# An encoder block whose attention products move one tile back, and two of whose attention outputs skip the trip through memory

## The chip, the core and the metric

The kernel runs on one core of one Trainium2 chip. The core has five engines with an instruction queue each: PE (matrix products), DVE and POOL (element-wise work), ACT (copies, exponentials, sigmoids) and SP, which here only issues transfers. An engine works off its queue in the order in which the program stands there, and waits on semaphores that the other engines and the transfers set. The metric is the device time of the whole program in microseconds (us); lower is better.

## The reference, cut to what matters

One encoder layer on 1024 tokens of width 1024:

```
a = rms_norm(x)
qa, ka, va, qd, kd, vd, gate_na, gate_dil = split(a @ w_in)
y_na  = neighborhood_attention(qa, ka, va)          # 8 heads of 64, 64-wide token grid
y_dil = dilated_attention(rotary(qd), rotary(kd), vd)   # 3 groups x 4 heads, groups merged per head
mixed = sigmoid(gate_na) * (y_na @ W_A) + sigmoid(gate_dil) * (y_dil @ W_B)
h = x + mixed @ W_o
h = h + relu(rms_norm(h) @ W_up)**2 @ W_down
h = h + sigmoid(rms_norm(h) @ W_g) * (p @ W_p)
out = rms_norm(h)
```

Everything is float32. The kernel gets that precision by splitting each operand into a rounded part and a remainder ("h" and "l", or "hi" and "lo") and adding up products of the parts.

## The kernel before

The program is written once, unrolled, and a scheduler puts the instructions of each engine in order by a simulated clock; only PE in the attention part, and a few marked instructions, keep the order in which they are written. Its stages: projections of q, k and v (0 to about 380 us of the span), attention (to about 725 us), the branch products with W_A and W_B (to about 810 us), then W_o, the MLP and the last gated embedding.

**The attention loop.** There are 160 tiles: 96 of the dilated attention (six pairs of heads, 16 tiles each), then 64 of the neighbourhood attention (eight heads, 8 tiles each). A tile is 128 queries of one head. For tile i the loop emits: the three scores ahead, that is the score product of tile i+3 (`na_score`, `dil_score`, lines 637 and 638, into a `sc` bank); the softmax of it on DVE (`soft`, `soft_max`, lines 644 to 655), ACT (the exponential, lines 647 and 657) and for the neighbourhood tiles POOL (`na_norm`, line 722, which scales the `s_sb` tile); the transposes of tile i on PE (`na_turn`, `dil_turn`, lines 731 and 860 to 866, into a `tp_p` bank), whose result ACT copies to `pt_h` and DVE subtracts to `pt_l` (`split`, lines 109 and 110). Two neighbourhood tiles, or four dilated ones, make a group; behind the last transposes of a group comes its product with v (`na_av`, lines 753 and 754, or `dil_av`, lines 900 and 903, into the single `av` bank), which needs all its `pt_h` and `pt_l`. ACT copies the upper half of that bank to `fold` (lines 762 and 908) and DVE adds it (lines 766 and 909) into the output tile, `y_na` or `numer`.

In iteration i PE is given, in this order: the transposes of tile i; some products of the gate projections (`ps_g`, line 602), dealt out as filler by `pay`; the scores of tile i+3; the product with v of a group that ended with tile i-1 (`late`); filler again; and the steps that were put off with `later`.

**Transfers around it.** All are issued by SP in one queue. `v_t` holds the v of a pair of heads (three buffers); `dil_v` loads its first part with the first score of a pair and its second part (`part` 1) in the turn of that pair's tile 1. `bias` has the neighbourhood bias. The four outputs of the neighbourhood attention (`y_na`, a tile for two heads) and the two merged outputs of the dilated attention (`y_d`, built by `dil_out` in three steps from `nm_d` and `fb_d`, tag `md`, two buffers, lines 964 and 968) share the tag `y` with two buffers. Each is stored to `y_scr` when it is done.

**The branch products.** Behind the loop the remaining filler runs; then all six outputs are loaded back from `y_scr` in the order 4, 5, 0, 1, 2, 3 (0 to 3 are the neighbourhood ones, 4 and 5 the dilated ones) into `y_raw` tiles of tag `y`, and split into the pairs `y_op` by ACT (line 109) and DVE (line 110). PE multiplies them with the branch weights (`ps_b`, lines 208 to 210): 288 products of 128x512, eight blocks f of output features by two halves of the tokens, 6 products for branch B (outputs 4 and 5) and 12 for branch A (0 to 3) in each. The gates come back from memory into `gt` tiles (the first half of the tokens in tag `bias`, the second in tag `md`); ACT takes the sigmoid, DVE multiplies `ps_b` by it (line 1058), and the `ps_b` bank is free only then (three banks).

Of the kernel before, what the change touches and what calls it, by code (L numbers as in the profile page):

```python
# [9 lines left out]
F32 = mybir.dt.float32  # L10
# [7 lines left out]
P = 128  # L18
S = 1024
# [13 lines left out]
AHEAD = 3  # L33
# [26 lines left out]
def encoder_kernel(ctx: ExitStack, tc: tile.TileContext, t: dict, out: bass.AP):  # L60
    nc = tc.nc
# [373 lines left out]
    with ExitStack() as st:  # L435
# [10 lines left out]
        raw, flips = {}, [0]  # L446
# [135 lines left out]
    with ExitStack() as st:  # L582
# [82 lines left out]
        def later(n, f):  # L665

            after.setdefault(now[0] + n, []).append(f)
# [66 lines left out]
        def na_av(h, cb, env):  # L734
            j, e = h // 2, h % 2
            pth, ptl = env.pop(("pt", cb))
            i_ = cb % 2
            if i_ == 0:
                env["av"] = ps_av.tile([P, 2, 256], F32, name="av", tag="av")
            av = env["av"]  # L740
            vh = [env["vt"][:, i_, gq, :] for gq in range(4)]
            first = True
            for gq, i, c in ((1, 0, None), (2, 1, None), (0, 2, 0), (3, 2, 1)):
                last = gq == 3
                if c is None:
                    mh = pth[:, i].rearrange("p a b -> p (a b)")
                    ml = ptl[:, i].rearrange("p a b -> p (a b)")
                    oc = slice(0, 256)
                else:
                    mh, ml = pth[:, i, c, :], ptl[:, i, c, :]  # L750
                    oc = slice(c * P, (c + 1) * P)
                m = P if last else 64
                pe(nc.tensor.matmul(av[:, i_, oc], vh[gq], mh, start=first, stop=False))
                pe(nc.tensor.matmul(av[0:m, i_, oc], vh[gq][:, 0:m], ml, start=False, stop=last))
                first = False
            if i_ == 0:
                return
            if e == 0 and cb == 1:
                na_y[j] = ap.tile([P, S], F32, name="y_na", tag="y")
            y = na_y[j]  # L760
            tmp = ap.tile([64, HALF], F32, name="fold", tag="fold", bufs=1)
            nc.scalar.copy(tmp, av[64:128].rearrange("p a b -> p (a b)"))
            for a in range(2):
                c = cb - 1 + a
                dst = y[e * 64:(e + 1) * 64].rearrange("p (r c) -> p r c", c=GW)[:, :, c * 16:(c + 1) * 16]
                nc.vector.tensor_tensor(dst, av[0:64, a].rearrange("p (r c) -> p r c", c=16),
                                        tmp[:, a * 256:(a + 1) * 256].rearrange("p (r c) -> p r c", c=16), op=ALU.add)
            if e == 1 and cb == 3:
                later(2, lambda: nc.sync.dma_start(y_scr[j], y))

        env_head = {}
# [73 lines left out]

        def dil_turn(g_, pr_, e, qi, pair, env):
            half, qp, qq = qi // 4, qi % 4 // 2, qi % 2
            if e == 0 and qi == 1:
                dil_v(g_, pr_, pair, 1)
            if qi % 4 == 0:  # L850
                env["pt"] = tuple(ap.tile([P, 8, P], F32R, name=f"pt_{b}", tag=f"pt_{b}") for b in "hl")
            if qq == 0:
                env["tp"] = ps_tp.tile([P, 4, P], F32, name="tp_p", tag="tp")
            pth, ptl = env["pt"]
            tp, pr = env["tp"], env.pop(("pr", qi))
            k0, n, _ = window(g_, qi)
            if g_ == 0:

                a0 = qi * P + 64 - k0
                pe(nc.tensor.transpose(tp[0:a0, 2 * qq, :], pr[:, 0:a0], ident))  # L860
                pe(nc.tensor.transpose(tp[0:n - a0, 2 * qq + 1, :], pr[:, a0:n], ident))
            elif g_ == 1:
                for b in range(2):
                    pe(nc.tensor.transpose(tp[:, 2 * b + qq, :], pr[:, b * P:(b + 1) * P], ident))
            else:
                pe(nc.tensor.transpose(tp[:, qq, :], pr[:, :P], ident))
            if qq == 0:
                return

            o0 = 4 * qp  # L870
            if g_ == 2:
                parts = ((2 * qp, 0, 2, P),)
            elif g_ == 0 and half == 0 and qp == 0:
                parts = ((o0, 0, 1, 64), (o0 + 1, 1, 3, P))
            elif g_ == 0 and half == 1 and qp == 1:
                parts = ((o0, 0, 3, P), (o0 + 3, 3, 1, 64))
            else:
                parts = ((o0, 0, 4, P),)
            for o, i, m, hh in parts:
                split(pth[:hh, o:o + m, :], ptl[:hh, o:o + m, :], tp[:hh, i:i + m, :])  # L880
# [71 lines left out]
        def dil_out(pr_, g_=0, y=None):  # L952

            y = y or ap.tile([P, S], F32, name="y_d", tag="y")
            nm = ap.tile([P, S], F32, name="nm_d", tag="md", bufs=2)
            nc.sync.dma_start(nm, n_scr[2 * g_ + pr_])
            fb = ap.tile([P, S], F32, name="fb_d", tag="md", bufs=2)
            for e in range(2):
                s_ = 2 * pr_ + e
                nc.sync.dma_start(fb[e * 64:(e + 1) * 64], f_scr[g_, s_:s_ + 1, :].broadcast_to((64, S)))  # L960

            def scaled():
                dst, a, b = (y, nm, fb) if g_ == 0 else (tok_view(fb, g_), nat_view(nm, g_), tok_view(fb, g_))
                tc.keep_in_program_order(nc.vector.tensor_tensor(dst, a, b, op=ALU.mult))

            def added():
                if g_:
                    tc.keep_in_program_order(nc.vector.tensor_tensor(y, y, fb, op=ALU.add))
                if g_ < 2:
                    dil_out(pr_, g_ + 1, y)  # L970
                else:
                    later(2, lambda: nc.sync.dma_start(y_scr[4 + pr_], y))

            later(5, scaled)
            later(6, added)
# [31 lines left out]
        for h in range(8):  # L1007
# [2 lines left out]
                after.setdefault(len(tiles) - 8, []).append(dil_merge)  # L1010
            elif h in (3, 5):
                after.setdefault(len(tiles) - (8 if h == 3 else 3), []).append(lambda pr_=h // 2 - 1: dil_out(pr_))
        late, i = None, -AHEAD
        while i <= len(tiles) or any(n >= i for n in after):
            if 0 <= i + AHEAD - 1 < len(tiles) and tiles[i + AHEAD - 1][0][3]:
                tiles[i + AHEAD - 1][0][3]()
            if 0 <= i < len(tiles):
# [3 lines left out]
            if i + AHEAD < len(tiles):  # L1021
                tiles[i + AHEAD][0][0]()
            now[0] = i
            if late:
                late()
            late = tiles[i][0][2] if 0 <= i < len(tiles) else None
            for f in after.pop(i, ()):
                f()
            pay(1.0)
# [7 lines left out]
            + [(ap, "pt_l", 2)] * 2  # L1037
        yt = {}
        for i, k in enumerate((4, 5, 0, 1, 2, 3)):
            raw = ap.tile([P, S], F32, name="y_raw", tag="y")  # L1040
            nc.sync.dma_start(raw, y_scr[k])
            yh, yl = (pool.tile([P, S], F32R, name="y_op", tag=tag, bufs=bufs)
                      for pool, tag, bufs in (spots[2 * i], spots[2 * i + 1]))
            split(yh, yl, raw)
            yt[k] = (yh, yl)
# [503 lines left out]
```

## Time and profile before

| | |
|---|---|
| time, median of three runs | 1675.5 us (1675.15, 1675.5 and one of 7496.38) |
| the profiled execution | 1673.03 us, span 1670.8 us |
| PE busy | 1571.5 us, 94% of the span |
| DVE, ACT, POOL busy | 1200.9, 708.4, 654.0 us |
| mean granted PE clock | 0.974 of full speed |
| moved by the transfers | 279.22 MB, 167 GB/s over the span |

The span runs from the first instruction to the last; the device time holds 2.2 us more. Two of the three runs agree within 0.35 us, and the third stands alone at more than four times that time. PE's busy time is modelled and includes time at the lower clock, so that 94% does not say that 6% is all that can be won. The full clock is 2.4 GHz and the lower level 1.2 GHz; a granted clock of 0.5 in a window means the lower level throughout.

### The profile page before, as it was taken

The page shows a single profiled execution, that of the slowest core. Times are in us where ns is not written, and L with a number is a line of the kernel's source. Part 1 is how long each engine was busy: PE and PEld are TensorE (multiplying, and loading weights), DVE is VectorE, ACT ScalarE, POOL GpSimd, SP SyncE. Part 2 cuts the span into 40 slices and gives each one's busy share as a digit, 9 for nine tenths or more (in the row PEclk, how much of TensorE's full clock was granted, in tenths as well). Part 3 has the DMA queues.
Part 4 walks back from the last instruction along what each step waited for, and adds up shares of the span by engine and source line. Part 5 has one row for each costly group of instructions (what it writes and reads, how often), then busy time and mean ns, then how long its engine had stood idle before and what let it go on. Part 6 is the DMA issues. An engine that isn't in the chain of part 4 may idle for free. (4 is left out here: it accounts for less than half of the span.)

```text
span 1670.8 us, 22589 instructions
## 1 busy us (share of the span) xinstructions
PE 1571.5 (94%) x7787; PEld 1312.3 (79%) x7787; DVE 1200.9 (72%) x2081; ACT 708.4 (42%) x1327; POOL 654.0 (39%) x434
## 2 busy tenths in 40 slices
PE   8899999999999998879997899999989999999997
PEld 7899777787787877757886688888877788887886
DVE  6744799734665788645557776777778999999955
ACT  7322222216787666644334333333345333333422
POOL 0233678613333222215304677777742322225100
PEclk9999999999999999989998999999999999999999
DMA  8552455674566778556343344434467454433122
GB/s 309 169 156 103 138 161 160 208 266 165 189 197 217 230 224 275 182 189 183 139 164 126 107 140 139 145 139 146 145 222 277 156 167 161 143 111 128 43 101 70
DMA packets 115058, 279.22 MB, mean 167 GB/s; under 512 B 14240, under 2 KB 30592, under 8 KB 114432
## 3 DMA queue, kind: packets, MB, share of 16 engines
q1 hardware_dynamic: 109184, 267.29, 48.7%
q10 hardware_dynamic: 5760, 10.49, 1.7%
q8 instruction: 62, 1.02, 0.3%
q14 instruction: 52, 0.43, 0.1%
HBM read 186.61 MB, written 91.11 MB: 166 GB/s over the span
## 5 line engine op out<-in xcount | busy, mean ns | idle before, releaser
L109 ACT CAST w_hi<-w_raw 128x512 fp32r<-128x512 f32 (+2 forms) x103 | 83.7, 826 | 144.4 <-POOL w_raw L470 55.9
L110 POOL TENSOR_TENSOR w_lo<-w_raw,w_hi 128x512 fp32r<-128x512 f32 (+2 forms) x33 | 64.2, 1947 | 154.5 <-ACT w_hi L109 150.5
L110 DVE TENSOR_TENSOR f_lo<-f_raw,f_hi 128x512 fp32r<-128x512 f32 x80 | 81.7, 1039 | 52.0 <-ACT f_hi L109 51.3
L110 DVE TENSOR_TENSOR w_lo<-w_raw,w_hi 128x1024 fp32r<-128x1024 f32 (+1 forms) x70 | 85.2, 1224 | 37.7 <-ACT w_hi L109 37.5
L722 POOL TENSOR_SCALAR s_sb<-s_sb,rs 128x384 f32<-128x384 f32 x64 | 41.3, 645 | 134.1 <-DVE rs L721 88.9
L109 ACT CAST f_hi<-f_raw 128x512 fp32r<-128x512 f32 x80 | 46.1, 613 | 82.9 <-DMA f_raw<-w_up 79.7
L110 DVE TENSOR_TENSOR pt_l<-tp_p,pt_h 128x384 fp32r<-128x384 f32 (+3 forms) x120 | 65.0, 543 | 15.4 <-ACT pt_h L109 14.8
L1172 POOL TENSOR_TENSOR u_t<-u_t 128x512 f32<-128x512 f32 x45 | 53.7, 1193 | 38.0 <-ACT u_t L1171 36.8
L109 ACT CAST pt_h<-tp_p 128x384 fp32r<-128x384 f32 (+3 forms) x120 | 56.1, 467 | 24.3 <-PE tp_p L731 14.5
L628 POOL TENSOR_TENSOR k_lo<-k_lo,k_st 128x1024 fp32r<-128x1024 f32 x12 | 33.2, 2767 | 76.1 <-ACT k_st L625 54.4
L1171 ACT ACTIVATE u_t<-u_t 128x512 f32<-128x512 f32 x45 | 28.4, 631 | 74.5 <-DVE u_t L1158 74.1
L1335 DVE TENSOR_TENSOR h<-ps_d,h 128x512 f32<-128x512 f32 x84 | 54.4, 678 | 1.7 <-PE ps_d L210 1.5
L637 PE MATMUL sc<-k_st,q_st 128*128 128x384 f32 (+3 forms) x160 | 53.0, 331 | 0.2 <-DVE stats L655 0.2
L657 ACT ACTIVATE s_sb<-s_sb,stats 128x256 f32<-128x256 f32 (+2 forms) x96 | 44.8, 468 | 19.3 <-DVE stats L655 18.9
L647 ACT ACTIVATE s_sb<-s_sb,nm 128x384 f32<-128x384 f32 x64 | 39.4, 616 | 31.2 <-DVE nm L646 31.0
L110 DVE TENSOR_TENSOR f_lo<-f_t,f_hi 128x512 fp32r<-128x512 f32 x32 | 51.3, 1608 | 1.8
L208 PE MATMUL ps_b<-y_op,w_hi 128*128 128x512 f32 x96 | 39.3, 419 | 11.2 <-ACT y_op L109 8.5
L638 PE MATMUL sc<-k_lo,q_st 128*128 128x384 f32 (+3 forms) x160 | 49.5, 310 | 0.0
L1335 DVE TENSOR_TENSOR sum_t<-ps_d,sum_t 128x512 f32<-128x512 f32 x72 | 46.6, 679 | 2.3 <-PE ps_d L210 2.3
L210 PE MATMUL ps_d<-w_hi,m_op 128*128 128x512 f32 x112 | 43.6, 399 | 2.7 <-DVE m_op L110 2.7
L496 POOL TENSOR_TENSOR o<-x,c 128x512 f32<-128x512 f32 x24 | 40.6, 1707 | 11.2 <-DVE c L491 8.7
L1297 POOL TENSOR_TENSOR t_raw<-pair,w_raw 128x1024 f32<-128x1024 f32 x6 | 15.6, 2598 | 75.0 <-DVE act11l L110 30.8
(478 smaller groups left out, 5826.3 us busy)
## 6 DMA issues: line engine op xcount, KB each, us to landing
f_raw<-w_up SPq DMA_DIRECT2D x32, 512.0 KB
w_raw<-w_in SPq DMA_DIRECT2D x26, 512.0 KB
u_raw<-l_scr SPq DMA_DIRECT2D x25, 512.0 KB
qk_scr<-o SPq DMA_DIRECT2D x96, 128.0 KB
h<-l_scr SPq DMA_DIRECT2D x24, 512.0 KB
l_scr<-u_t SPq DMA_DIRECT2D x42, 256.0 KB
l_scr<-u_s SPq DMA_DIRECT2D x42, 256.0 KB
w_raw<-w_qk SPq DMA_DIRECT2D x20, 512.0 KB
```

What stands on the lines that cost most here:

```text
L109: nc.scalar.copy(hi, src)
L110: eng.tensor_tensor(lo, src, hi.bitcast(F32), op=ALU.subtract)
L208: nc.tensor.matmul(ps, sh, mh, start=first, stop=False)
L210: nc.tensor.matmul(ps, sl, mh, start=False, stop=last)
L496: nc.gpsimd.tensor_tensor(dst, x, y, op=op)
L637: pe(nc.tensor.matmul(o, qs[:, qsl], kk, start=True, stop=False))
L638: pe(nc.tensor.matmul(o, qs[:, qsl], ll, start=False, stop=True))
L647: nc.scalar.activation(s_[:, :n], s_[:, :n], AF.Exp, bias=nm, scale=1.0, accum_out=sm)
L657: nc.scalar.activation(s_[:, :n], s_[:, :n], AF.Exp, bias=nm, scale=-1.0, accum_out=sm)
L722: nc.gpsimd.tensor_scalar(pr, pr, rs, 1.0, op0=ALU.mult, op1=ALU.mult)
L1172: nc.gpsimd.tensor_tensor(c, c, c, op=ALU.mult)
L1335: nc.vector.tensor_tensor(d, ps, d, op=ALU.add)
```

## The change

The product with v of a group moves from one tile behind the group's last transposes to two: `late` becomes a list of two entries, and the loop runs one more iteration. The second part of `dil_v` is loaded in the turn of tile 2 of a pair and no longer of tile 1. Two of the six outputs, 3 (the last neighbourhood one) and 5 (the second dilated one), are not stored to `y_scr` and loaded again: their own tiles of tag `y` are split directly. The other four are still loaded, into `y_raw` tiles of tag `md` in place of `y`.

```diff
-            if e == 1 and cb == 3:
+            if e == 1 and cb == 3 and j < 3:
                 later(2, lambda: nc.sync.dma_start(y_scr[j], y))
...
-            if e == 0 and qi == 1:
+            if e == 0 and qi == 2:
                 dil_v(g_, pr_, pair, 1)
...
                 if g_ < 2:
                     dil_out(pr_, g_ + 1, y)
+                elif pr_ == 0:
+                    later(2, lambda: nc.sync.dma_start(y_scr[4], y))
                 else:
-                    later(2, lambda: nc.sync.dma_start(y_scr[4 + pr_], y))
+                    na_y[5] = y
...
-        late, i = None, -AHEAD
-        while i <= len(tiles) or any(n >= i for n in after):
+        late, i = [None, None], -AHEAD
+        while i <= len(tiles) + 1 or any(n >= i for n in after):
...
-            if late:
-                late()
-            late = tiles[i][0][2] if 0 <= i < len(tiles) else None
+            if late[0]:
+                late[0]()
+            late = [late[1], tiles[i][0][2] if 0 <= i < len(tiles) else None]
...
-            raw = ap.tile([P, S], F32, name="y_raw", tag="y")
-            nc.sync.dma_start(raw, y_scr[k])
+            if k in (3, 5):
+                raw = na_y[k]
+            else:
+                raw = ap.tile([P, S], F32, name="y_raw", tag="md", bufs=2)
+                nc.sync.dma_start(raw, y_scr[k])
```

Line numbers of the kernel below line 971 grow by 2 to 6. In the lists that follow, a bracket names the semaphores that an instruction waits for: an engine's, or a transfer's (DMAHW).

PE near the end of the neighbourhood attention, before: a score, the product with v (line 753 with `pt_h`, line 754 with `pt_l`), filler.

```order
L637 MATMUL sc<-k_st,q_st 128x384 [waits PE_49]
L638 MATMUL sc<-k_lo,q_st 128x384
L753 MATMUL av<-pt_h,v_t 128x256 [waits DMAHW1_49,Activation_49]
L754 MATMUL av<-pt_l,v_t 64x256 [waits DVE_49]
L753 MATMUL av<-pt_h,v_t 128x256
L754 MATMUL av<-pt_l,v_t 64x256
L753 MATMUL av<-pt_h,v_t 128x128
L754 MATMUL av<-pt_l,v_t 64x128
L753 MATMUL av<-pt_h,v_t 128x128
L754 MATMUL av<-pt_l,v_t 128x128
L602 MATMUL ps_g<-act01h,w_hi 128x512
```

The same place now:

```order
L637 MATMUL sc<-k_st,q_st 128x384 [waits PE_49]
L638 MATMUL sc<-k_lo,q_st 128x384
L602 MATMUL ps_g<-act01h,w_hi 128x512
L602 MATMUL ps_g<-act01l,w_hi 128x512
L602 MATMUL ps_g<-act01h,w_lo 128x512
L731 MATMUL tp_p<-ident,s_sb 128x128 [waits Pool_49]
L731 MATMUL tp_p<-ident,s_sb 128x128 x2
L602 MATMUL ps_g<-act01h,w_hi 128x512
L602 MATMUL ps_g<-act01l,w_hi 128x512
L602 MATMUL ps_g<-act01h,w_lo 128x512
L753 MATMUL av<-pt_h,v_t 128x256 [waits DMAHW2_49,Activation_49]
L754 MATMUL av<-pt_l,v_t 64x256
```

Between the score and the product with v now stand six filler products and the three transposes of the next tile, and the first `pt_l` product has no wait for DVE of its own any more.

SP where the attention loop ends, before:

```order
L139 DMA w_raw<-w_br 128x768 [waits DMAHW4_49,DMAHW0_49,Pool_49]
L1051 DMA gt<-g_scr 128x2x512 [waits DMAHW7_49,DMAHW1_49,DVE_49]
L972 DMA y_scr<-y_d 128x1024 [waits DMAHW2_49,DVE_49]
L1051 DMA gt<-g_scr 128x2x512 [waits DMAHW3_49]
L769 DMA y_scr<-y_na 128x1024 [waits DVE_49]
L1041 DMA y_raw<-y_scr 128x1024 [waits DMAHW5_49,DMAHW2_49]
L139 DMA w_raw<-w_br 128x768 [waits DMAHW7_49,DMAHW6_49,Pool_49]
L1041 DMA y_raw<-y_scr 128x1024 [waits DMAHW4_49,DMAHW0_49]
```

And now:

```order
L139 DMA w_raw<-w_br 128x768 [waits DMAHW6_49,Pool_49]
L139 DMA w_raw<-w_br 128x768 [waits DMAHW4_49,DMAHW0_49,Pool_49]
L1047 DMA y_raw<-y_scr 128x1024 [waits DMAHW7_49,DMAHW1_49,DVE_49]
L1047 DMA y_raw<-y_scr 128x1024 [waits DMAHW2_49,DVE_49]
L1047 DMA y_raw<-y_scr 128x1024 [waits DMAHW3_49,DMAHW1_49,DVE_49]
L1047 DMA y_raw<-y_scr 128x1024 [waits DMAHW5_49,DMAHW2_49,DVE_49]
L139 DMA w_raw<-w_br 128x768 [waits DMAHW6_49,Pool_49]
L1057 DMA gt<-g_scr 128x2x512 [waits DMAHW7_49,DMAHW3_49,DVE_49]
L1057 DMA gt<-g_scr 128x2x512 [waits DMAHW5_49,DMAHW0_49,DVE_49]
```

The two stores (lines 972 and 769) are gone; the loads of `y_raw` stand where a load of `gt` stood and wait for other buffers; the two loads of `gt` stand behind all four of them.

ACT at the same place, before, from the last `fold` copy:

```order
L762 COPY fold<-av 64x512 [waits DVE_49,PE_49]
L1052 ACTIVATE gt<-gt 128x1024 [waits DMAHW2_49,DMAHW1_49,DVE_49]
L109 CAST w_hi<-w_raw 128x768 [waits DMAHW6_49,PE_49]
L604 COPY g_st<-ps_g 128x512 [waits PE_49]
L605 DMA g_scr<-g_st 128x512 [waits Activation_49]
L1052 ACTIVATE gt<-gt 128x1024 [waits DMAHW3_49,DMAHW2_49,DVE_49]
L109 CAST y_op<-y_raw 128x1024 [waits DMAHW5_49]
L109 CAST y_op<-y_raw 128x1024 [waits DMAHW0_49]
```

And now:

```order
L762 COPY fold<-av 64x512 [waits DVE_49,PE_49]
L109 CAST y_op<-y_d 128x1024 [waits DVE_49]
L109 CAST y_op<-y_na 128x1024 [waits DVE_49]
L109 CAST y_op<-y_raw 128x1024 [waits DMAHW1_49]
L109 CAST y_op<-y_raw 128x1024 [waits DMAHW2_49]
L109 CAST w_hi<-w_raw 128x768 [waits DMAHW6_49,PE_49]
L604 COPY g_st<-ps_g 128x512 [waits PE_49]
L605 DMA g_scr<-g_st 128x512 [waits Activation_49]
L109 CAST y_op<-y_raw 128x1024 [waits DMAHW3_49]
L109 CAST y_op<-y_raw 128x1024 [waits DMAHW5_49]
L1058 ACTIVATE gt<-gt 128x1024 [waits DMAHW7_49,DVE_49]
```

The splits of the two outputs that stay in place come first and wait for DVE alone; the sigmoid of `gt` has moved behind all six splits.

The order on all engines is the same as before up to the attention loop, and behind the branch products but for five exchanges of neighbouring rows on PE, DVE and ACT.

## Rows read from the trace of the kernel before

**Rows 1.** Windows by stage: busy us (count) per engine, granted clock, DMA share, GB/s

```profile
380.00:540.00 160.00, 148.47 (x871) 123.56 (x870) 94.33 (x285) 121.76 (x316) 49.66 (x19) 0.96 0.57 186
540.00:725.00 185.00, 167.56 (x957) 142.02 (x955) 136.60 (x401) 118.95 (x259) 44.88 (x66) 0.96 0.71 227
725.00:810.00 85.00, 72.86 (x290) 56.75 (x290) 43.66 (x54) 36.22 (x44) 31.89 (x21) 0.90 0.53 165
```

**Rows 2.** PE's waits, 380 to 725 us: total us, times, longest

```profile
PE tp_p L731 <- POOL s_sb L722: 8.7, 5, 4.1
PE av L900 <- ACT pt_h L109: 5.2, 5, 2.2
PE av L754 <- DVE pt_l L110: 4.1, 6, 1.7
PE av L903 <- DVE pt_l L110: 3.5, 6, 1.5
PE av L753 <- ACT pt_h L109: 2.7, 3, 1.2
```

**Rows 3.** Timeline at two waits for an attention product: start, us, what, idle before

```profile
389.24 0.51 ACT L657 ACTIVATE s_sb<-s_sb,stats 128x256 f32<-128x256 f32 x1
...
391.31 0.39 PE L900 MATMUL av<-pt_h,v_t 128*128 128x256 f32 x1 [2.25 <-ACT pt_h L109]
...
683.91 0.59 POOL L722 TENSOR_SCALAR s_sb<-s_sb,rs 128x384 f32<-128x384 f32 x1 [6.30 <-DVE rs L721]
...
684.25 0.33 PE L754 MATMUL av<-pt_l,v_t 128*64 128x256 f32 x1 [1.73 <-DVE pt_l L110]
```

**Rows 4.** Windows of 4 us behind three waits, columns as in Rows 1

```profile
392.00:396.00 4.00, 3.96 (x15) 3.17 (x16) 1.03 (x2) 1.37 (x4) 2.21 (x1) 0.66 0.44 144
...
424.00:428.00 4.00, 3.49 (x12) 2.76 (x13) 1.14 (x2) 0.59 (x2) 1.94 (x1) 0.50 0.78 256
428.00:432.00 4.00, 4.00 (x19) 3.42 (x18) 1.40 (x5) 1.66 (x6) 0.00 (x0) 0.65 0.03 10
...
700.00:704.00 4.00, 2.34 (x9) 1.98 (x10) 4.00 (x9) 1.87 (x5) 0.59 (x1) 0.56 0.46 136
```

**Rows 5.** Timeline where the attention loop ends and the branch products begin

```profile
719.53 0.38 SPq L1051 DMA_DIRECT2D gt<-g_scr  x1
719.95 1.22 DVE L968 TENSOR_TENSOR y_d<-y_d,fb_d 128x1024 f32<-128x1024 f32 x1
...
721.65 0.75 DVE L766 TENSOR_TENSOR y_na<-av,fold 64x256 f32<-64x256 f32 x2 [0.48 <-ACT fold L762]
...
724.52 0.39 PE L602 MATMUL ps_g<-act11l,w_hi 128*128 128x512 f32 x1
...
724.75 0.39 PE L602 MATMUL ps_g<-act11h,w_lo 128*128 128x512 f32 x1
725.33 1.06 ACT L1052 ACTIVATE gt<-gt 128x1024 f32<-128x1024 f32 x1 [3.72 <-DMA gt<-g_scr]
...
726.72 0.32 SPq L1041 DMA_DIRECT2D y_raw<-y_scr  x1
...
730.58 1.04 ACT L109 CAST y_op<-y_raw 128x1024 fp32r<-128x1024 f32 x1 [1.33 <-DMA y_raw<-y_scr]
731.66 1.23 DVE L110 TENSOR_TENSOR y_op<-y_raw,y_op 128x1024 fp32r<-128x1024 f32 x1 [9.26 <-ACT y_op L109]
...
731.68 0.79 PE L208 MATMUL ps_b<-y_op,w_hi 128*128 128x512 f32 x1 [6.54 <-ACT y_op L109]
```

**Rows 6.** One window from the last gate product to the last split

```profile
725.00:748.60 23.60, 14.13 (x42) 9.38 (x42) 9.24 (x9) 9.69 (x10) 1.81 (x1) 0.71 0.62 202
```

**Rows 7.** ACT's waits, 380 to 725 us: copies behind attention products

```profile
ACT fold L762 <- PE av L754: 11.5, 9, 3.3
ACT fold L908 <- PE av L903: 7.9, 11, 2.6
```

**Rows 8.** The transfer queue's waits, 540 to 760 us: loads of v

```profile
SPq L694 <- PE av L754: 25.7, 9, 4.6
```

## The prediction

> **What bounds the kernel now.** PE is the busiest engine, and what the change touches lies between 380 and 810 us, so I first read the windows of that stretch [rows 1]. PE is busy for 148.47 of 160 us, 167.56 of 185 and 72.86 of 85, while DVE and ACT have a quarter or more of their time free in each. So PE sets the pace and loses time in two ways: in waits, and at a granted clock of 0.96, 0.96 and 0.90. At full speed the same work would be shorter by about 0.04 x 160 = 6.4 us, 0.04 x 185 = 7.4 us and 0.10 x 85 = 8.5 us.
>
> Next come PE's waits in the attention loop [rows 2]. The products with v wait for their own group's `pt_h` (5.2 and 2.7 us) and `pt_l` (4.1 and 3.5 us): 15.5 us in 20 waits. The largest other wait is that of the transposes for POOL's scaled scores, 8.7 us. The reader should see both: they hang on the same DVE and ACT queues, one is what the change attacks, the other is where PE stands next.
>
> Last, the timeline where the loop ends [rows 5]. PE starts its last filler product at 724.75, 0.23 us after the one ahead of it (the step of a 512-wide product at full clock), and ends it at 725.14. The first branch product starts at 731.68, after 6.54 us of idling: it waited for a load of output 4 issued at 726.72, which ACT took up at 730.58. In the 23.6 us from 725 to 748.6 PE gets through 42 products at a clock of 0.71 [rows 6]. At 0.23 us they take 42 x 0.23 = 9.7 us, so 13.9 us are lost there, half in that one gap and the rest in later loads and the low clock.
>
> **The products with v, one tile later.** No instruction is added. Between the last transposes of a group and its product now lies one more tile of PE work: 160/96 = 1.7 us in the dilated part, 185/64 = 2.9 us in the other [rows 1]. None of the waits was longer than 2.25 us [rows 2, 3], so the wait at the product itself should mostly go. What is late next is the transposes of the following tile, and two cases show how much comes back.
>
> At 391.31 the product had waited 2.25 us for `pt_h`, since 389.06 [rows 3]. PE would now go on with three fillers (0.7 us) and the next transposes, whose exponential ended at 389.24 + 0.51 = 389.75, as PE arrives. It meets the product 1.7 us later than before, at about 390.8, and waits 0.5 us: some three quarters are won. At 684.25 it had waited 1.73 us for `pt_l`, since 682.52 [rows 3]. Three fillers later, at 683.2, it would stand before transposes whose scores POOL scales until 683.91 + 0.59 = 684.50. So 1.3 of 1.73 us come back and a quarter is won: DVE is late for both. Waits for `pt_h` are 7.9 us and for `pt_l` 7.6 us [rows 2], so I take 0.75 x 7.9 + 0.25 x 7.6 = 7.8, that is 8 us.
>
> The clock adds to it. Behind the waits near 391, 423 and 700 it is granted at 0.66, 0.50 and 0.65, and 0.56 in windows of 4 us [rows 4]: 1.4 + 3.4 + 1.8 = 6.6 us of full-speed time lost. A shorter gap may or may not spare a fall; I take 2 of the 6.6. The term is **10 us**, with bounds 0 (every wait comes back at the transposes) and 15.5 + 6.6 = 22 us.
>
> **What moves along.** The second half of a pair's v is loaded one tile later and used one tile later, so I cost it at nothing. If that cover were gone, it would be a tile in the two pairs whose first half already needs it, 2 x 1.7 = 3.4 us. In the neighbourhood part SP stands for 25.7 us in nine waits until a product with v frees a `v_t` buffer [rows 8], with biases, keys and weights queued behind. These waits end up to one tile later now. I cost that at nothing too, since none of PE's larger waits names a transfer [rows 2]; the price without that cover is in the rivals.
>
> **Two outputs kept, four loaded elsewhere.** Two stores and two loads of 512 KB go, and with them the wait of the first load for the buffer that a store held. The new chain, worked out with the durations in [rows 5]: SP can issue the load of output 4 where it issued a gate load, at 719.53. A load of this size took 730.58 - 726.72 = 3.9 us, or 725.33 - 719.53 = 5.8 us among others; I take 4.9, so it lands at 724.4. ACT first splits outputs 5 and 3, which DVE has ready at 719.95 + 1.22 = 721.17 and 721.65 + 0.75 = 722.40. Then it takes output 4 until 724.4 + 1.04 = 725.4, and PE starts 0.3 us after its filler in place of 6.54. DVE's half (1.23 us) ends at 726.6; PE, two products in, waits 0.8 us for it. Then ten products fill the time to 729.0, and output 0, loaded from 721.17 on, is split by 728.4. Outputs 1 and 2 need the `md` buffers of 4 and 0, free at 726.6 and 728.4. Output 1 lands at 731.5, ACT is through at 732.5, DVE at 733.8: PE, out of work at 730.3, waits 2.2 and 0.8 us. Output 2 follows 1.8 us behind and costs 0.4 us. The waits are 0.3 + 0.8 + 2.2 + 0.8 + 0.4 = 4.5 us, and the 41 branch products of that window end at 725.1 + 41 x 0.23 + 4.5 = 739.1 in place of 748.6: 9.5 us. From that I take 1 us, since the second half's gates now follow output 1 into the same buffers and hold a `ps_b` bank, and the clock may fall near 731. The term is **8.5 us**. Above it lies 13.9 us (nothing waits). Below, loads at 5.8 us in two links cost 1.8 us more, two windows at the 0.66 of [rows 4] 2.8 us, a late gate 1.5 us: 9.5 - 6.1 = 3.4 us.
>
> The Trainium skill ("DMA: Bandwidth & Descriptors", section "Issuing engines are not separate DMA queues") says that all transfers run on the same 16 engines and interleave. By it the 5.8 us among other loads would hold for each, the term would be 1.8 us less and the time about 1659; the two landings above agree with it, but with two stores gone fewer are in flight.
>
> **The sum.** 10 + 8.5 = 18.5 us. Against the profiled execution, 1673.03 us, that gives 1654.5; it lies 2.5 us under the median of the runs, of which two agree and the third is left out. Against the median I predict 1675.5 - 18.5 = **1657 us**, 1.1% faster.
>
> **Rivals.** *The wait only changes its place.* All 15.5 us come back at the transposes and only the end of the loop gains: 1675.5 - 8.5 = 1667. The case at 684 speaks for it, the one at 391 against.
>
> *Everything is hidden.* 22 + 13.9 = 35.9 us, 1639.6. For it speaks that ACT and DVE have free time in every stage [rows 1]; against it, that the transposes' 8.7 us are untouched and outputs 1 and 2 must wait for two buffers.
>
> *Slower: the `fold` copy blocks ACT.* It stands in ACT's queue ahead of exponentials and `pt_h` casts, and the product that it waits for now comes a tile later. ACT already stood 11.5 + 7.9 = 19.4 us before 20 of the 40 copies [rows 7]. If the other 20 now hold it as long, and PE pays that one for one and wins nothing at the products, the time is 1675.5 - 8.5 + 19.4 = 1686.4. It decides when ACT's stand is longer than the lead of the scores, three tiles or 5 to 9 us; the longest so far was 3.3 us, which speaks against it. The same with SP's queue: nine waits a tile longer, 9 x 2.9 = 26 us, 1693.
>
> The Trainium skill ("Perfetto Trace Analysis", section "Tensor Engine Instruction (MATMUL, LD_WEIGHTS)") says that ACT, DVE and GpSimd are strict FIFO and only PE reorders a little. By it this rival would hold wherever a copy stands ahead of work that is due, up to its 1686.4; the stands before the copies agree with the rule, none shows PE paying.
>
> **How the numbers follow.** The forecast, 1648 to 1664, has 0.55; the wait that changes its place, 1664 to 1672, 0.20; everything hidden, under 1648, 0.15; slower, up to about 1693 and in a worse case more, 0.10. Leaving a tenth out on either side, the range is **1640 to 1672**. A measurement of this kernel can tell about 2%, 33.5 us, from no change. Faster by over 2% (under 1642) is two thirds of the third case, 0.10. Slower by over 2% (over 1709) needs both queues at once, 0.02. Within 2% is the rest, 0.88.
>
> **What the profile after would show.** PE's waits for `pt_h` and `pt_l` at the products under 4 us together, and the waits at the transposes grown by up to 8 us; if they grow by 15, the first rival holds. The first branch product within 1 us of the last filler, two waits of 1 to 3 us in the next 10 us, and the clock near 1. ACT's waits at `fold` about as long as before; much more, with longer waits of PE for exponentials, would be the slower rival. The prediction is wrong if the load of output 4 doesn't start near the end of `fb_d`'s last use, or if PE falls to the low clock in attention more often than before.

## The result, and the profile after

The changed kernel takes 1651.3 us (median of four runs, 1647.51 to 1654.93), the kernel before beside it 1675.3 us. The medians lie 24 us apart; the ratio, 0.9872 with a 95% interval of 0.985 to 0.9894, makes it 21 us (18 to 25). The prediction was 1657 us, range 1640 to 1672. The execution that was profiled is the slowest of the four: 1654.93 us, span 1653.1 us. So the profile shows 1670.8 - 1653.1 = 17.7 us of the gain. In a second profile of the same kernel the span is 1648.1 us.

To see where they lie I cut both spans at the start of the same four pieces of work: the first score, the first transposes of the neighbourhood part, the last product with v, and the last branch product. The columns are the window, PE's busy us (instructions), granted clock, DMA share, GB/s. Before:

```profile
381.90:542.80 160.90, 149.37 (x876) 0.96 0.57 188
542.80:720.70 177.90, 160.46 (x925) 0.96 0.71 224
720.70:809.60 88.90, 76.77 (x310) 0.90 0.55 171
```

After:

```profile
383.80:530.00 146.20, 140.91 (x876) 1.00 0.63 203
530.00:711.50 181.50, 162.35 (x926) 0.94 0.71 224
711.50:791.00 79.50, 72.72 (x309) 0.98 0.52 163
```

Each row holds the same products in both kernels, but for one filler that has changed its side at the last product with v. So the change of a row splits into PE's idling and PE's busy time:

| stretch | length | of it idling | of it busy time |
|---|---|---|---|
| dilated part | -14.7 us | 11.5 to 5.3: -6.2 | -8.5 |
| neighbourhood part | +3.6 us | 17.4 to 19.1: +1.7 | +1.9 |
| branch products | -9.4 us | 12.1 to 6.8: -5.3 | -4.1 |

These make -20.5 us. The attention loop starts 1.9 us later and what follows the branch takes 0.9 us more (862.1 against 861.2), which leaves the 17.7.

Busy time grows where the clock is low, but not all of its fall is the clock. In windows of 10 us of the dilated part (columns as above) these are below full clock before:

```profile
390.00:400.00 10.00, 8.35 (x39) 0.83 0.44 156
...
420.00:430.00 10.00, 6.82 (x27) 0.70 0.55 183
430.00:440.00 10.00, 9.67 (x58) 0.96 0.07 27
...
530.00:540.00 10.00, 8.40 (x42) 0.83 0.47 164
```

They lose 1.7 + 3.0 + 0.4 + 1.7 = 6.8 us of full-speed time, and after the change none is below 1.00. So 6.8 of the 8.5 us are the clock, and what the other 1.7 are is not settled. In the neighbourhood part the same sum is 6.8 us before (windows at 0.83, 0.98, 0.85, 0.66) and 10.2 after (0.66, 0.92, 0.74, 0.66).

PE's waits from 380 to 725 us, total us, times, longest, against [rows 2]:

```profile
PE tp_p L731 <- POOL s_sb L722: 15.1, 8, 4.4
PE sc L638 <- POOL k_lo L628: 2.7, 3, 1.2
PE av L753 <- ACT pt_h L109: 1.8, 1, 1.8
PE tp_p L731 <- DVE nm L646: 1.7, 1, 1.7
...
PE av L754 <- DVE pt_l L110: 0.2, 1, 0.2
```

The products' waits of 15.5 us are down to 2.0, and the 1.8 is that of the very last group, behind which no tile is left. The dilated part has none any more. In the neighbourhood part the transposes have taken them over: 15.1 us for POOL's scaling in place of 8.7.

In the changed kernel's windows of 10 us the clock shows where those waits are:

```profile
640.00:650.00 10.00, 5.53 (x32) 0.92 0.79 269
650.00:660.00 10.00, 10.00 (x49) 0.74 0.66 197
...
690.00:700.00 10.00, 6.45 (x24) 0.66 0.68 194
```

A mean of 0.66 or 0.74 is a mix of the two levels, 2.4 and 1.2 GHz. PE had stood for 4.35 us ahead of 649.56, and in the next 10 us gets through 49 products; busy windows at full clock hold 57 to 65 there. From 380 to 580 us no 10-us window of the changed kernel is below 1.00.

What was late at 649.56, in the timeline of that place (start, us, engine, what, idle before):

```profile
640.03 2.02 DVE L964 TENSOR_TENSOR fb_d<-nm_d,fb_d 128x1024 f32<-128x1024 f32 x1
...
643.07 1.22 DVE L627 SCALAR_TENSOR_TENSOR q_st<-q_raw,q_st 64x1024 fp32r<-64x1024 f32 x1
...
644.32 0.55 DVE L644 CUSTOM_DVE_ANT_0 s_sb<-bias,sc 128x384 f32<-128x384 f32 x1
...
644.80 1.22 DVE L628 TENSOR_TENSOR k_lo<-k_lo,k_st 128x1024 fp32r<-128x1024 f32 x1
...
646.40 0.14 DVE L646 TENSOR_SCALAR nm<-mx 128x1 f32<-128x1 f32 x1
646.47 1.21 DVE L968 TENSOR_TENSOR y_d<-y_d,fb_d 128x1024 f32<-128x1024 f32 x1
646.64 0.62 ACT L647 ACTIVATE s_sb<-s_sb,nm 128x384 f32<-128x384 f32 x1 [0.81 <-DVE nm L646]
...
648.60 0.15 DVE L721 RECIPROCAL rs<-sm 128x1 f32<-128x1 f32 x1
...
648.92 0.58 POOL L722 TENSOR_SCALAR s_sb<-s_sb,rs 128x384 f32<-128x384 f32 x1 [6.06 <-DVE nm L646]
...
649.56 0.90 PE L731 MATMUL tp_p<-ident,s_sb 128*128 128x128 f32 x3 [4.35 <-POOL s_sb L722]
```

The wait is put down to POOL, but POOL had idled for 6 us. One tile's small steps stand in DVE's queue between large ones: its maximum is there at 644.88, the sign change that the exponential needs starts at 646.40, behind the 1.22 us of the next head's `k_lo` and a `pt_l`; the exponential and its sum are through at 647.35, the reciprocal starts at 648.60, behind the merge's addition, another `pt_l` and the next tile's maximum. Nothing of this depends on where the product with v stands.

The end of the loop, against [rows 5]:

```profile
707.48 2.63 DVE L964 TENSOR_TENSOR fb_d<-nm_d,fb_d 128x1024 f32<-128x1024 f32 x1
...
710.13 9.01 SPq L1047 DMA_DIRECT2D y_raw<-y_scr  x4
...
712.27 1.05 ACT L109 CAST y_op<-y_d 128x1024 fp32r<-128x1024 f32 x1
...
714.18 1.05 ACT L109 CAST y_op<-y_raw 128x1024 fp32r<-128x1024 f32 x1
...
715.50 0.39 PE L602 MATMUL ps_g<-act11h,w_lo 128*128 128x512 f32 x1
...
715.73 0.39 PE L208 MATMUL ps_b<-y_op,w_hi 128*128 128x512 f32 x1
...
717.59 0.50 PE L208 MATMUL ps_b<-y_op,w_hi 128*128 128x512 f32 x1 [1.48 <-ACT y_op L109]
...
722.68 0.50 PE L209 MATMUL ps_b<-y_op,w_hi 128*128 128x512 f32 x1 [0.44 <-DVE y_op L110]
...
724.15 1.04 ACT L109 CAST y_op<-y_raw 128x1024 fp32r<-128x1024 f32 x1 [2.78 <-DMA y_raw<-y_scr]
```

The first branch product follows the last filler after one step, 0.23 us, where 6.54 us were lost. The second stands for 1.48 us: it is already one of output 0.

### The profile page after: what moved, and what is told of

Read it like the earlier page. It is cut to its first block, busy times and chain, and to the rows that moved or that the text cites. A ratio compares the mean times of both kernels' runs of the same rounds, so it can differ in the third digit from the quotient of the medians.

```text
span 1653.1 us, 22585 instructions
## 1 busy us (share of the span) xinstructions
PE 1561.5 (94%) x7787; PEld 1308.2 (79%) x7787; DVE 1193.6 (72%) x2081; ACT 708.4 (43%) x1327; POOL 652.6 (39%) x434
## 5 line engine op out<-in xcount | busy, mean ns | idle before, releaser
L731 PE MATMUL tp_p<-ident,s_sb 128*128 128x128 f32 x192 | 33.9, 288 | 17.1 <-POOL s_sb L722 15.1
L731 PEld LDWEIGHTS tp_p<-ident,s_sb 128*128 128x128 f32 x192 | 25.1, 147 | 29.9 <-POOL s_sb L722 20.4
L644 DVE CUSTOM_DVE_ANT_0 s_sb<-bias,sc 128x384 f32<-128x384 f32 x64 | 35.1, 548 | 15.8 <-PE sc L638 14.1
```

The source lines that it names most:

```text
L644: nc.vector.tensor_tensor_reduce(s_[:, :n], bias, sc[:, :n], 1.0, -3.0e38, op0=ALU.subtract, op1=ALU.max, accum_out=mx)
L731: pe(nc.tensor.transpose(tp[:, i * P:(i + 1) * P], pr[:, kb * P:(kb + 1) * P], ident))
```

## The experiments

Each kernel was timed in five rounds against the kernel before on the same chip. A "stretch" is one of the three rows above. The first four tell the two halves of the change apart.

**The same kernel again.** No edit.

> The changed kernel once more, for its spread: 1647 to 1655 us, ratio to the kernel before 0.985 to 0.989, PE's waits at the products with v under 4 us. If the 24 us of the first comparison hold a lucky clock, the ratio comes out at 0.99 or above.

1651.28 us, ratio 0.9873 (0.985 to 0.9896). Stretches 146.3, 179.3, 78.7 us. The difference repeats; in this execution the neighbourhood part lost 1.4 us and not 3.6.

**Only the later product.** The outputs are stored and loaded as before.

```diff
-            if e == 1 and cb == 3 and j < 3:
+            if e == 1 and cb == 3:
...
-            if k in (3, 5):
-                raw = na_y[k]
-            else:
-                raw = ap.tile([P, S], F32, name="y_raw", tag="md", bufs=2)
-                nc.sync.dma_start(raw, y_scr[k])
+            raw = ap.tile([P, S], F32, name="y_raw", tag="y")
+            nc.sync.dma_start(raw, y_scr[k])
```

> Only the product with v one tile later (and the second part of dil_v); all six outputs stored and loaded through the old buffers. Theory (two independent parts, the loop worth 11 us by the landmarks of the two traces, its dilated part 15 and its neighbourhood part -4): about 1664 us, ratio 0.993, the first branch product still 6 to 7 us behind the last filler. Rival (the gain is nearly all at the end of the loop, the rest is the clock of one execution): 1672 us or more, ratio above 0.998.

1657.58 us, ratio 0.9902 (0.9883 to 0.992). Stretches 147.7, 179.8, 85.3 us. That is 6 us less time than the theory gave. The first branch product still stands for 7.01 us, as it said.

**Only the outputs.** The product stays one tile behind.

```diff
-        late, i = [None, None], -AHEAD
+        late, i = None, -AHEAD
...
-            late = [late[1], tiles[i][0][2] if 0 <= i < len(tiles) else None]
+            late = tiles[i][0][2] if 0 <= i < len(tiles) else None
```

> Only the other handling of the outputs, products with v one tile behind as before. Theory: about 1666 us, ratio 0.9945, first branch product within 1 us of the last filler, loop as long as before. Rival (the end gains only because the loop ahead of it runs smoother): 1671 us or more.

1663.4 us, ratio 0.9937 (0.9915 to 0.9959). Stretches 160.9, 178.6, 78.1 us. So the loop's gain belongs to the later product and most of the branch's to the outputs. The two gains by their ratios, 16.4 and 10.6 us, add up to 27, the whole change gives 21; the intervals are 3 to 4 us wide to each side, so that this difference is not settled. One overlap is in the rows: with the later product alone the branch stretch is 3.6 us shorter already, though its start is not (below).

**Two tiles behind in the dilated part, one in the other.**

```diff
             late = [late[1], tiles[i][0][2] if 0 <= i < len(tiles) else None]
+            if i > 96:
+                late = [late[0] or late[1], None]
```

> The changed kernel, but the products of the neighbourhood tiles one tile behind again; those of the dilated tiles stay two behind. Theory (in the neighbourhood part every wait comes back at the transposes, since DVE is late for both): as fast as the changed kernel or up to 4 us faster, 1647 to 1652 us, and the waits at the products of that part return at 5 to 9 us while those at its transposes fall by as much. Rival (the second tile helps there too and the longer stretch in the trace was the clock): 5 us or more slower than the changed kernel, 1656 us and above.

1647.25 us, ratio 0.9836 (0.9811 to 0.9861), 4 us under the changed kernel by the medians; the intervals overlap. Stretches 147.8, 177.8, 78.3 us. PE's waits in the neighbourhood part:

```profile
PE tp_p L731 <- POOL s_sb L722: 7.5, 4, 4.1
PE av L754 <- DVE pt_l L110: 3.8, 5, 1.7
```

They are back at the products, much as [rows 2]. There the later product won nothing. All profiles with three tiles of lead and the whole arithmetic say the same: the neighbourhood part takes 177.8 to 178.6 us, 16.0 to 17.4 of it idling, where its product stands one tile behind (three kernels), and 178.0 to 181.5 us, 17.7 to 19.2 of it idling, where it stands two behind (six profiles). The time between two bursts of DVE is given out at one place or the other.

**Which half of the output handling pays.** First all six outputs go through memory again, but by the merge's buffers; then two are kept, and the four loads go into y's buffers.

```diff
-            if k in (3, 5):
-                raw = na_y[k]
-            else:
-                raw = ap.tile([P, S], F32, name="y_raw", tag="md", bufs=2)
-                nc.sync.dma_start(raw, y_scr[k])
+            raw = ap.tile([P, S], F32, name="y_raw", tag="md", bufs=2)
+            nc.sync.dma_start(raw, y_scr[k])
```

> All six attention outputs are stored and loaded back as before the change, but the loads go into the merge's two buffers and not into y's; the later product with v stays. Theory A (the buffers: before, the loads waited for the y buffers that the last tiles hold, and the stage started behind them): at least two thirds of the 9.4 us between the last product with v and the last branch product stays, so this stretch is 79 to 83 us and the time 1651 to 1655. Theory B (the two round trips that are left out carry it): the stretch goes back to 86 to 89 us and the time to 1658 to 1661.

```diff
-                raw = ap.tile([P, S], F32, name="y_raw", tag="md", bufs=2)
+                raw = ap.tile([P, S], F32, name="y_raw", tag="y")
```

> The changed kernel with the two outputs kept in place, but the four loads go into y's buffers as before the change and not into the merge's. With the run that loads all six through the merge's buffers (last product with v to last branch product 85.5 us, against 79.5 in the changed kernel and 88.9 before) it splits the gain at the branch. Theory A (most of the gain is that two of six outputs need no trip, the buffers add little): 79 to 82 us and a time of 1650 to 1654. Theory B (both halves are needed, the loads must not wait for y's buffers): 84 us or more and a time of 1655 to 1660.

All six through the merge's buffers: 1656.12 us, ratio 0.9895 (0.9872 to 0.9918), branch stretch 85.5 us, between the two theories and nearer to B. Two kept, loads into y's buffers: 1652.18 us, ratio 0.9873 (0.9852 to 0.9895), 79.9 us, as A had it. PE's waits from 709 to 798 us in the first:

```profile
PE ps_b L208 <- ACT y_op L109: 6.1, 3, 4.5
...
PE ps_b L209 <- DVE y_op L110: 2.7, 5, 0.8
```

and from 711 to 795 us in the second:

```profile
PE ps_b L208 <- ACT y_op L109: 2.9, 1, 2.9
...
PE ps_b L209 <- DVE y_op L110: 1.3, 2, 0.8
```

The first branch product comes 4.7 us behind the last product with v in the first kernel and 8.9 in the second, and yet the second one's stretch is 5.6 us shorter. A prompt start is not what counts: six loads through two buffers go on holding PE up after it (8.8 us in eight waits), four loads that start late cost 4.2 us in three. The last of the six outputs is split 24.1 us behind the last product with v in the first kernel and 18.9 in the second.

Both kernels hold the later product too, so the run with that alone (85.3 us) is what they are to be set against: the buffers bring nothing there, the skipped trips 5.4 us. The window from the end of the last filler to the end of the 41st branch product, the work of [rows 6], tells it without the rest of the stretch: before, all six through the merge's buffers, two kept with y's buffers, and the whole change:

```profile
725.14:748.77 23.63, 14.17 (x42) 0.71 0.61 200
714.71:738.42 23.71, 13.53 (x42) 0.86 0.59 186
716.18:732.35 16.17, 12.01 (x43) 0.89 0.44 148
715.89:731.80 15.91, 12.10 (x42) 0.89 0.55 174
```

With the later product alone it is 23.9 us. So the skipped trips win here what is won, and neither the buffers nor the later product does. The 3.6 us by which the later product alone shortens the stretch lie behind this window; these rows don't settle what they are.

**Where the neighbourhood part's waits come from.** A fourth tile of lead; its control (`g_st` with two buffers, which made the room); then less work on DVE.

```diff
-AHEAD = 3
+AHEAD = 4
...
-                    gs = ap.tile([P, HALF], F32, name="g_st", tag="g_st", bufs=3)
+                    gs = ap.tile([P, HALF], F32, name="g_st", tag="g_st", bufs=2)
...
-            s_ = aa.tile([P, 384], F32, name="s_sb", tag="s_sb", bufs=4)
+            s_ = aa.tile([P, 384], F32, name="s_sb", tag="s_sb", bufs=5)
```

> The changed kernel with scores and their softmax issued four tiles ahead of the transposes and not three (one more score buffer in SBUF, one buffer fewer for the gates' staging). Theory A (the neighbourhood part's waits at the transposes, 16.8 us in it, come from bursts of VectorE work at the change of a head and in the merge, which delay one tile's softmax): one more tile in hand absorbs most of them, waits of the transposes for GpSimd's scaling fall to 6 us or less and the part from 181.5 to 173 or less, the time to 1643 or less. Theory B (VectorE and GpSimd have too little throughput over this part, or the scaling is queued late whatever the lead): the waits fall by less than 4 us and the time stays within 3 us of 1651.

> The changed kernel with two staging buffers for the gates in place of three and nothing else: the control for the runs with a fourth tile of lead, which needed that room. If the lead alone made those faster: within 3 us of 1651, not faster. If the buffer had a part in it: 3 us or more below 1651.

The lead: 1647.42 us, ratio 0.9845 (0.9822 to 0.9869), neighbourhood part 174.1 us. The control: 1652.04 us, ratio 0.9881 (0.9859 to 0.9902), neighbourhood part 178.0 us, so the buffer has no part in the gain of time. The row of waits for POOL's scaling, 15.1 us in the changed kernel and 15.4 in the control

```profile
PE tp_p L731 <- POOL s_sb L722: 15.4, 8, 4.3
```

is gone with the lead, and other steps of DVE and ACT have taken much of its place:

```profile
PE tp_p L731 <- DVE pt_l L110: 3.9, 2, 2.7
PE tp_p L731 <- DVE nm L646: 2.8, 2, 2.2
PE av L753 <- ACT pt_h L109: 2.6, 2, 1.8
```

Between the theories: the part is 7.4 us shorter than in the first profile of the changed kernel, in which it was the longest of all (2.9 of it idling, 4.5 busy time), and 3.9 us shorter than in the control. The longest wait is 2.7 us and not 4.4. The time fell by 4 us, not by the 8 of theory A.

The merge's arithmetic left out (the dilated outputs are neither weighted nor added but in 8 columns, and the first part of each is loaded straight into `y`, which spares a buffer of the merge; the rows of lines 964 and 968 show 16.1 us of arithmetic in the part, on 128x1024, and not the 12 on 128x512 that the expectation says):

```diff
-            nm = ap.tile([P, S], F32, name="nm_d", tag="md", bufs=2)
+            nm = ap.tile([P, S], F32, name="nm_d", tag="md", bufs=2) if g_ else None
-            nc.sync.dma_start(nm, n_scr[2 * g_ + pr_])
+            nc.sync.dma_start(nm if g_ else y, n_scr[2 * g_ + pr_])
...
-                dst, a, b = (y, nm, fb) if g_ == 0 else (tok_view(fb, g_), nat_view(nm, g_), tok_view(fb, g_))
-                tc.keep_in_program_order(nc.vector.tensor_tensor(dst, a, b, op=ALU.mult))
+                a, b = (nm, fb) if g_ else (y, fb)
+                tc.keep_in_program_order(nc.vector.tensor_tensor(b[:, :8], a[:, :8], b[:, :8], op=ALU.mult))
...
-                    tc.keep_in_program_order(nc.vector.tensor_tensor(y, y, fb, op=ALU.add))
+                    tc.keep_in_program_order(nc.vector.tensor_tensor(y[:, :8], y[:, :8], fb[:, :8], op=ALU.add))
```

> The changed kernel without the merge's arithmetic: the dilated outputs are not weighted and added (VectorE's multiplications and additions of 128x512 are cut to 8 columns, some 12 us of VectorE inside the neighbourhood part); its loads, stores and order stay. Theory A (the transposes' waits in the neighbourhood part stand behind bursts of VectorE work, the merge's being the largest): waits of the transposes there fall from 16.8 to 9 us or less, the part from 181.5 to 173 or less. Theory B (they come from elsewhere, the operands of the next head or GpSimd's own queue): the part is within 3 us of 181.5.

1637.89 us, ratio 0.979 (0.9767 to 0.9813). The keys' low half left out in all but 8 columns:

```diff
-            (nc.vector if h < 8 else nc.gpsimd).tensor_tensor(kl, kf, ks.bitcast(F32), op=ALU.subtract)
+            w = slice(0, 8 if h < 8 else S)
+            (nc.vector if h < 8 else nc.gpsimd).tensor_tensor(kl[:, w], kf[:, w], ks[:, w].bitcast(F32), op=ALU.subtract)
```

> The changed kernel without most of the low half of the keys in the neighbourhood part: VectorE's subtraction of 128x1024 at each of the eight changes of head is cut to 8 columns (some 1.15 us less each, 9 us in all). Theory A (the transposes' waits stand behind VectorE's bursts; without the merge's arithmetic 11.1 us of them were left, of the heads' own): waits of the transposes fall from 16.8 us to 12 or less and the part from 181.5 us to 176 or less. Theory B (the rest of the waits has nothing to do with VectorE): within 2 us of 181.5.

1644.9 us, ratio 0.9837 (0.9815 to 0.986). The neighbourhood part without the merge's arithmetic, window, PE busy, clock, DMA share, GB/s:

```profile
528.80:697.70 168.90, 157.01 (x925) 0.98 0.75 244
```

and without the keys' low half:

```profile
528.20:699.00 170.80, 156.43 (x925) 0.98 0.76 238
```

12.6 and 10.7 us shorter than in the first profile of the changed kernel, 9.1 and 7.2 us shorter than the 178.0 of the control. The whole kernel is 13.4 and 6.4 us faster by its medians. DVE's busy time in the part, 133 of 181.5 us, falls by 13.8 and 6.7 us, so the gain is about as large as the work left out, though DVE stood idle for a quarter of the part. The transposes' waits fall from 16.8 us to 11.1 and to 12.1 (11.2 for POOL, 0.9 for `nm`). So both bursts are on PE's path, as theory A had it for the length; the sum of waits fell less than it said for the merge, and the rest of the gain stands in PE's busy time, 157.01 and 156.43 us for 162.35, at a clock of 0.98 for 0.94. The spared buffer of the first run was not tried by itself.

**A faster version, and one more step from it.** The product one tile behind in the neighbourhood part, with the fourth tile of lead; then that with the merge's arithmetic on POOL.

```diff
-AHEAD = 3
+AHEAD = 4
...
             late = [late[1], tiles[i][0][2] if 0 <= i < len(tiles) else None]
+            if i > 96:
+                late = [late[0] or late[1], None]
```

> The version that beat the changed kernel (the product with v two tiles behind in the dilated part alone, one tile behind in the neighbourhood part; outputs as in the change) with scores issued four tiles ahead. If one more tile of lead absorbs VectorE's bursts, its neighbourhood part falls from 177.8 us to 172 or less and the time from 1647 to 1642 or less; if the waits at the product (3.8 us for the low half of the probabilities, which the lead does not touch) and throughput set it, it stays within 3 us of 1647.

```diff
-                tc.keep_in_program_order(nc.vector.tensor_tensor(dst, a, b, op=ALU.mult))
+                tc.keep_in_program_order(nc.gpsimd.tensor_tensor(dst, a, b, op=ALU.mult))
...
-                    tc.keep_in_program_order(nc.vector.tensor_tensor(y, y, fb, op=ALU.add))
+                    tc.keep_in_program_order(nc.gpsimd.tensor_tensor(y, y, fb, op=ALU.add))
```

> The fastest version so far (four tiles of lead, two tiles behind in the dilated part alone, 1640.5) with the merge's ten multiplications and additions of 128x1024 on GpSimd, which is busy 43 of 182 us in the neighbourhood part, and not on VectorE, where they take 15.6 us by their rows. If VectorE's bursts still cost time there: the part falls from 170.1 to 166 us or less, the time to 1636 or less. If GpSimd's own scaling, queued behind operations of 2.4 us or more, takes the place of that: the part is 172 us or more and the time 1642 or more. Between these the two cancel.

The first: 1640.5 us, ratio 0.9801 (0.9778 to 0.9824), faster than both kernels. The run without the merge's arithmetic, at 1637.89, is not clear of it by the intervals. The neighbourhood part is 170.1 us, the branch stretch 76.6. The second: 1640.24 us, ratio 0.9806 (0.9784 to 0.9829), neighbourhood part 173.4 us, branch stretch 75.5. The part is 3.3 us longer, as the second theory had it, and the time is the same, as the last sentence allowed; what makes up for the part is not settled by these rows.

## Why the prediction came out as it did

The forecast, 1657, lies 5.7 us above the median and the change is faster by 1.3%, inside the case that had 0.55. In the profiles the two terms hold as wholes: 11.1 us in the loop for 10, 9.4 at the branch for 8.5. Taken singly they were both too small, since the later product alone gives 16.4 us and the outputs alone 10.6; that 18.5 came so near the 21 of the whole is in part luck. Inside the first term, two errors cancelled.

**The step that failed: the size of the waits and the clock in the loop.** The term was 8 us of waits and 2 us of clock. Measured: idling 6.2 - 1.7 = 4.5 us, busy time 8.5 - 1.9 = 6.6 us, of which the granted clock accounts for 6.8 - 3.4 = 3.4. The 6.6 us of lost clock that the 2 were taken from hold three places only; by the windows of 10 us the loop had lost 6.8 + 6.8 = 13.6. The split by releaser, three quarters of the waits for `pt_h` and one quarter of those for `pt_l`, came from one example of each, and each example stood in another part of the loop. What decides is the part. In the dilated part the waits for both went, all 8.7 us, and with them its falls of the clock. In the neighbourhood part nothing was won, for `pt_h` or `pt_l`: there the first rival holds, and the case at 684 was the one to generalise. The run with the later product in the dilated part alone shows it: no slower than the whole change (4 us faster by the medians), with a neighbourhood part as long as before.

**What the places showed of the predicted signs.** Waits at the products 2.0 us, under the 4 foretold. The waits for POOL's scaling have grown by 6.4 us, within "up to 8". A wait that no step had: scores for `k_lo`, 2.7 us in three, in the dilated part, where POOL makes it (2.4 to 3.4 us each by its row). "ACT's waits at `fold` about as long as before" was wrong the good way; against [rows 7]:

```profile
ACT fold L762 <- PE av L754: 5.3, 5, 1.6
ACT fold L908 <- PE av L903: 3.0, 6, 0.7
```

19.4 us became 8.3, so the slower rival had its sign wrong. The runs place it: with the outputs alone ACT stands 11.6 + 7.9 us, with the later product alone 4.7 + 3.2, and with the later product in the dilated part alone 13.6 us for the neighbourhood copies and 3.4 for the dilated ones. So each part's later product shortens that part's stand. My reading of why, not tested by itself, is that ACT stood there because PE stood in the product, and stands less once PE meets the product without waiting. The Trainium skill ("Perfetto Trace Analysis", section "Tensor Engine Instruction (MATMUL, LD_WEIGHTS)") has these engines strictly in order; the rows agree with it, ACT standing up to 1.6 us before a copy, but the rule alone gives no price: that hangs on when what is waited for comes. The queue of SP did stand longer, against [rows 8]:

```profile
SPq L694 <- PE av L754: 36.9, 12, 6.1
```

and none of PE's waits in the loop names a transfer: costed at nothing, rightly.

**The branch.** The chain came out nearly as worked out. The load of output 4 was issued at 710.13, when `fb_d`'s last use ended (707.48 + 2.63 = 710.11). ACT took it up 4.05 us later, straight behind another split and without standing for it, so that it had landed by then (I had 4.9). The waits in the first 12 us were 0, 1.48, 0.44, 1.37 and 0.52, 3.8 us for 4.5. The gates hold a `ps_b` bank for 3.0 us in two waits, 2.7 before, all behind these 12 us, so they added next to nothing. The clock did: at 0.89 over the window, the 41st branch product ends 15.9 us behind the last filler, where 14.0 and 1 us set aside made 15.0. In the second profile of the same kernel it is 12.2. The Trainium skill ("DMA: Bandwidth & Descriptors", section "Issuing engines are not separate DMA queues") has all transfers interleave on the same 16 engines. The trace agrees for the last of the four loads: issued at about 718.8 behind another, it was taken up at 724.15, after ACT had stood 2.78 us for it, 5.3 us. The first, at most 4.05 us, shows that the 5.8 us which the prediction drew from the page do not hold for each. But the reason that I put first, the early issue of output 4, is not the main one: with the late issue and the two trips spared the stretch is 79.9 us, with the early issue and all trips 85.5, and with neither, but the later product, 85.3.

**What stays open.** The clock of one execution differs from the next (neighbourhood part 181.5 and 179.3 us in two profiles of the same kernel), so the 3.6 us lost there are 0.1 to 3.6 over the six profiles of such a part. Why the two halves give less together than apart was not settled, nor why the merge on POOL wins nothing.

## What to carry to other kernels

Moving a consumer later wins what it waited for only if the engine that feeds it has caught up by then; look at each stage by itself, and at what that feeder does ahead of the wait, before taking one example as the rule. Where a stage waits on a feeder that is 73% busy, look for lumps in its queue: with DVE busy for 6.7 us less, in lumps of 1.2 us, the kernel was 6.4 us faster. And count the idling of a stretch and its busy time for the same instructions separately, since half of what a stall costs may be the clock behind it.

## What the runs showed of the hardware that was not expected

The low clock cost as much as the stalls that went before it: in the dilated part 6.8 us of full-speed time were lost to it before and none after, against 6.2 us less idling. None of the waits for the products there was longer than 2.25 us. Over the neighbourhood part the clock was 0.94 with a longest wait of 4.4 us, 0.96 in the control with 4.3, and 0.97 with 2.7, so these rows don't show that the longest wait alone sets it.

A multiplication or addition of 128x1024 on VectorE has two prices in one kernel: 1.21 to 1.23 us with plain operands (lines 628, 968 and two of line 964; one took 1.39) and 1.97 to 2.63 us with a strided view of the columns (line 964, four of its six).
